# Hybrid encoder block on one core: t stores issued seven half products behind, accumulators copied at the end of their own product, a fifth hi buffer, and a PSUM copy of the rounded part for every weight operand

## The chip, the cores and the metric

The kernel runs on one core of one Trainium2 chip, as one program. The time is device microseconds of that core. The kernel before was run three times: the median is 2214.05 us, the lowest 2213.38 us, the highest 2215.1 us. One more execution was profiled; the engine rows and the trace are of that one.

## What is computed

One layer of a hybrid encoder in float32, for 512 tokens of width 2048: a normalisation and one input projection whose columns feed three head groups (stick-breaking attention, a convolution module, a spatial gating module), a per-head normalisation, an output projection with residual, and then the feed-forward part, in which most of the time lies:

```python
h = rms_norm(x, ffn_norm[l])
gate = causal_depthwise_conv(jnp.einsum('bsd,df->bsf', h, w_gate[l]), ffn_conv_w[l], ffn_conv_b[l])   # 3 taps
up = jnp.einsum('bsd,df->bsf', h, w_up[l])
x = x + jnp.einsum('bsf,fd->bsd', jax.nn.silu(gate) * up, w_down[l])                                   # d_ff = 5632
return rms_norm(x, final_norm)
```

## The kernel before, in words

**Split operands.** TensorE multiplies in a rounded float32 format. Each operand is therefore split in two: `hi` is the rounded value, a cast on ScalarE (ACT), and `lo = src - hi` is the remainder, a subtraction on VectorE (DVE). `mm3` (line 276) adds three matmuls: hi·hi, hi·lo, lo·hi. The weights are split as they come in: `w_split` (line 250) for the input and output projections, `make_split` (line 1022) for gate and up, `dn_split` (line 1180) for down. All three take their hi tile from a ring `whi` of four buffers and their lo tile from a ring `wlo` of four.

**Stages.** Input projection, convolution and attention work run until about 590 us of the span, the output projection until 771 us, gate and up from 771 to 1725 us, down and the last normalisation until the end.

**Gate and up.** There are 44 groups of 256 columns, in turn of w_gate and of w_up (44 = 22 pairs of a gate group and an up group). Each group is one Strassen-like product: seven products over half-size blocks (`SEQ`, line 990), each in two halves over the contraction. Such a half product is called a unit here: 14 units in a group, numbered 0 to 13, 12 matmuls of 256 columns each, on the weight operands L11 (units 0, 1), S1 (2, 3), L12 (4, 5), S3 (6, 7), S2 (8, 9), S4 (10, 11), L22 (12, 13). An L operand is raw weight from a DMA buffer (`b_raw`); an S operand is a sum that GpSimd (POOL) makes (`make_sum`, line 1008) into a ring of three tiles (`b_sum`). The other side of the matmul (`ra`, `rb`, `rc`, `rd`) is the split activation, made once.

The remainder of an S operand, and of L11, is taken from a second copy of the rounded value: ACT casts once to the hi tile in SBUF and once to a PSUM tile `b_hp`, and DVE subtracts the PSUM copy. For L12 and L22 there is only the one cast, and DVE reads both inputs from SBUF:

```python
if (i == 0 and g > 0) or SEQ[i][0] in SUMS:
    hp = zz("b_hp").rearrange("p (k c) -> p k c", k=4)
    act_.copy(hi, src)
    act_.copy(hp.bitcast(F32R), src)
    vec.tensor_tensor(out=lo, in0=src, in1=hp, op=ALU.subtract)
else:
    split(hi, lo, src)
```

**Accumulators.** A group has two PSUM banks (`pt`) of two halves each: X and Y in the first, Z1 and Z2 in the second. The seven products accumulate into X, Z1, Y, Z2, X, Z1, Z2. `product` (line 1078) issues the matmuls and, behind certain products, the copies and additions into two SBUF tiles `ff_g` (c11, c12 in the first, c21, c22 in the second; ring `tmp_g` of eight). Matmuls into one half of a bank wait for reads of either half that were issued before them.

**Outputs.** `gate_out` (line 1046) multiplies a gate tile by a row of norms, runs the three-tap convolution (one ACT operation, two DVE operations that read SBUF twice, `ff_c`) and the SiLU on ACT, and one multiplication on POOL. `up_out` (line 1068) multiplies the up tile by it on POOL (`ff_g<-ff_g,ff_c`), and ACT's queue then issues its store to the DRAM tensor `t`. Both are generators: `run_steps` (line 1118) advances each by one `yield` per unit, which sets how many units behind each step stands.

**Order.** The loop at line 1221 issues, for each unit, the sum of six units ahead, the split of four units ahead, the unit's matmuls and the output steps. A scheduler then orders each engine's instructions by its own estimate of when they are ready; ACT keeps the order of the code. The order that came out is what each engine executes, each engine in its own queue, one behind the other.

Of the kernel before, what the change touches and what calls it, by code (L numbers as in the profile page):

```python
# [9 lines left out]
F32 = mybir.dt.float32  # L10
F32R = mybir.dt.float32r  # L11
# [3 lines left out]
P = 128  # L15
S = 512
# [4 lines left out]
NF = DFF // P  # L21
# [4 lines left out]
TAPS = 31  # L26
# [87 lines left out]
def trunk_kernel(  # L114
# [16 lines left out]
    act_, vec, pool = iss.scalar, iss.vector, iss.gpsimd  # L131

    const = ctx.enter_context(tc.tile_pool(name="const", bufs=1))
    up_stage, gating_stage = ExitStack(), ExitStack()
    wp = ctx.enter_context(tc.tile_pool(name="wp", bufs=3))
# [7 lines left out]
    def s2k(name, dt=F32):  # L143
        return sb.tile([P, S], dt, tag="s2k", bufs=NS2K, name=name)
# [41 lines left out]
    ident = const.tile([P, P], F32, name="ident")  # L186
    make_identity(nc, ident)

    rows_m = const.tile([16, P], F32, name="rows_m")
    nc.scalar.dma_start(out=rows_m, in_=mix_norm[0].rearrange("(k p) -> k p", p=P))  # L190

    def columns(rows, n, name):
# [41 lines left out]
    def w_load(i):  # L234
        if i < len(plan):
            src, k0, nk, c0, ncol = plan[i]
            raws[i] = wp.tile([P, nk, ncol], F32, tag="raw", bufs=3, name="w_raw")
            nc.sync.dma_start(
                out=raws[i],
                in_=src[k0 * P : (k0 + nk) * P, c0 : c0 + ncol].rearrange("(k p) c -> p k c", p=P),  # L240
            )

    def split(hi, lo, src, hi_eng=None, lo_eng=None):
        if hi_eng is None:
            act_.copy(hi, src)
        else:
            hi_eng.tensor_copy(hi, src)
        return (lo_eng or vec).tensor_tensor(out=lo, in0=src, in1=hi.bitcast(F32), op=ALU.subtract)

    def w_split(j):  # L250

        i, s = divmod(j, 2)
        if i >= len(plan):
            return
        nk, ncol = plan[i][2] // 2, plan[i][4]
        hi = wp.tile([P, nk, ncol], F32R, tag="whi", bufs=4, name="w_hi")
        lo = wp.tile([P, nk, ncol], F32R, tag="wlo", bufs=4, name="w_lo")
        iss.now -= 1.5
        split(hi, lo, raws[i][:, s * nk : (s + 1) * nk, :])
        iss.now += 1.5  # L260
        halves[j] = (hi, lo)
        if s == 1:
            del raws[i]
            w_load(i + 3)
# [16 lines left out]
    def proj_t(h, hook=None):  # L281

        banks = [mm("pt") for _ in range(2)]
        for kt in range(KT):
            kk = kt % 2
            if kk == 0:
                hi, lo = w_next()
            for m in range(2):
                cs = slice(m * P, (m + 1) * P)
                mm3(banks[m], hi[:, kk, cs], lo[:, kk, cs], h[kt][0], h[kt][1], kt == 0, kt == KT - 1)  # L290
                if m == 0:
                    iss.tick()
            if kk == 0:
                w_ahead()
            if hook:
                hook(kt)
            iss.tick()
        return banks
# [104 lines left out]
    for b in range(4):  # L403
# [2 lines left out]
            nc.sync.dma_start(out=xblk[b][tt], in_=x[tt * P : (tt + 1) * P, b * S : (b + 1) * S])  # L406
        if b < 3:
            w_load(b)
    rows_a = const.tile([48, P], F32, name="rows_a")
    for i, v in enumerate((merge_norm, ffn_norm)):  # L410
        nc.sync.dma_start(out=rows_a[16 * i : 16 * i + 16, :], in_=v[0].rearrange("(k p) -> k p", p=P))
    for i, v in enumerate((conv_b, conv_ln_g, conv_ln_b, sg_v_norm)):
        nc.sync.dma_start(out=rows_a[32 + 4 * i : 36 + 4 * i, :], in_=v[0].rearrange("(k p) -> k p", p=P))
    rows_c = const.tile([TAPS * 4, P], F32, name="rows_c")
    nc.sync.dma_start(out=rows_c, in_=conv_w[0].rearrange("k (c p) -> (k c) p", p=P))
    rows_f = [const.tile([2 * NF, P], F32, name=f"rows_f{i}") for i in range(2)]
    nc.sync.dma_start(out=rows_f[0], in_=ffn_conv_w[0, 0:2].rearrange("k (c p) -> (k c) p", p=P))
    nc.sync.dma_start(out=rows_f[1][0:NF, :], in_=ffn_conv_w[0, 2].rearrange("(c p) -> c p", p=P))
    nc.sync.dma_start(out=rows_f[1][NF : 2 * NF, :], in_=ffn_conv_b[0].rearrange("(c p) -> c p", p=P))
# [149 lines left out]
    def by_row(banks, name):  # L569
        res = [s2k(name) for _ in banks]  # L570
        for m, t in enumerate(res):
            w = vec.tensor_tensor(out=t, in0=banks[m], in1=row1[0], op=ALU.mult)
        return res, w

    for half in range(2):
# [4 lines left out]
        a_sb, _ = by_row(banks, "cv_a")  # L580
# [261 lines left out]
    for half in range(2):  # L842
        u, _ = by_row(proj_t(hT, first_operands if half else None), "sg_u")
# [35 lines left out]
    def blk_load(g):  # L879
        if g < len(groups):  # L880
            src, c0 = groups[g]
            for h in range(2):
                for q in range(2):
                    t = raw_pool.tile([P, 4, 256], F32, tag="raw", bufs=6, name="b_raw")
                    k0 = (8 * h + 4 * q) * P
                    nc.sync.dma_start(
                        out=t, in_=src[k0 : k0 + 4 * P, c0 : c0 + 256].rearrange("(k p) c -> p k c", p=P)
                    )
                    blk[g, h, q] = t
# [26 lines left out]
    def halves_of(t):  # L916
        return t[:, 0:HT], t[:, HT:S]
# [40 lines left out]
    for nb in range(4):  # L958
# [32 lines left out]
    SEQ = (  # L991
        ("L11", "R11"), ("S1", "T1"), ("L12", "R21"), ("S3", "T3"), ("S2", "T2"), ("S4", "R22"), ("L22", "T4"),
    )
# [6 lines left out]
    def operand(g, name, q):  # L1000
        return raw_block(g, name, q) if name[0] == "L" else sums[g, name, q]

    SUMS = {
        "S1": ("L21", "L22", ALU.add), "S3": ("L11", "L21", ALU.subtract),
        "S2": ("S1", "L11", ALU.subtract), "S4": ("L12", "S2", ALU.subtract),
    }
# [15 lines left out]
    def make_split(n):  # L1022
        g, i, q = UNITS[n]
        if i == 0 and q == 0 and g > 0:
            blk_load(g + 1)
        hi = wp.tile([P, 4, P], F32R, tag="whi", bufs=4, name="b_hi")
        lo = wp.tile([P, 4, P], F32R, tag="wlo", bufs=4, name="b_lo")
        src = operand(g, SEQ[i][0], q)
        if (i == 0 and g > 0) or SEQ[i][0] in SUMS:


            hp = zz("b_hp").rearrange("p (k c) -> p k c", k=4)
# [5 lines that stand above are left out]
        parts[n] = (hi, lo)  # L1038
# [29 lines left out]
    def up_out(f, c):  # L1068
        yield
        pool.tensor_tensor(out=c, in0=c, in1=sil.pop(f), op=ALU.mult)  # L1070
        yield
        yield
        nc.scalar.dma_start(out=t_dram[f // 2][:, f % 2, :], in_=c)

    AHEAD, SUM_AHEAD = 4, 6
# [2 lines left out]
    def product(n):  # L1078
        g, i, q = UNITS[n]
        if g not in banks_of:  # L1080
            b1, b2 = mm("pt"), mm("pt")
            banks_of[g] = (*halves_of(b1), *halves_of(b2))
        X, Y, Z1, Z2 = banks_of[g]
        acc = (X, Z1, Y, Z2, X, Z1, Z2)[i]
        hi, lo = parts.pop(n)
        for kk in range(4):
            rh, rl = R[SEQ[i][1], 4 * q + kk]
            mm3(acc, hi[:, kk, :], lo[:, kk, :], rh, rl, i < 2 and q == 0 and kk == 0, q == 1 and kk == 3)
        if q == 0:
            return  # L1090
        if i < 2:
            return
        if g not in outs_of:
            outs_of[g] = (tmp_g("ff_g0"), tmp_g("ff_g1"))
        (c11, c12), (c21, c22) = (halves_of(c) for c in outs_of[g])
        f0 = 2 * (g // 2)
        out_fn = gate_out if g % 2 == 0 else up_out
        if i == 2:
            act_.copy(c11, X)
            vec.tensor_tensor(out=c11, in0=c11, in1=Y, op=ALU.add)  # L1100
        elif i == 3:
            vec.tensor_copy(c22, Z1)
            vec.tensor_tensor(out=c22, in0=c22, in1=Z2, op=ALU.add)
        elif i == 4:
            u_of[g] = tmp("ff_u")[:, 0:HT]
            act_.copy(u_of[g], X)
            vec.tensor_tensor(out=c22, in0=c22, in1=X, op=ALU.add)
        elif i == 5:
            vec.tensor_tensor(out=c12, in0=u_of[g], in1=Z1, op=ALU.add)
            out_steps.append(out_fn(f0, outs_of[g][0]))  # L1110
        elif i == 6:
            vec.tensor_tensor(out=c21, in0=u_of[g], in1=Z2, op=ALU.add)
            out_steps.append(out_fn(f0 + 1, outs_of[g][1]))
# [66 lines left out]
    def dn_split(j):  # L1180
        i, s = divmod(j, 2)
        if i >= len(dplan):
            return
        if j < n_steps:
            hi = wp.tile([P, S], F32R, tag="whi", bufs=4, name="w_hi")
            lo = wp.tile([P, S], F32R, tag="wlo", bufs=4, name="w_lo")
        else:
            hi, lo = big("w_hi"), big("w_lo")
        split(hi, lo, raw_d[i][:, s, :])
        halves_d[j] = (hi, lo)  # L1190
        if s == 1:
            del raw_d[i]
            dn_load(i + 5)
# [50 lines left out]
    for kg in range(4):  # L1244
        for nb in range(4):
# [4 lines left out]
            for f in range(10 * kg, 10 * kg + 10):  # L1250
# [8 lines left out]
                hi, lo = halves_d.pop(j)  # L1259
# [12 lines left out]
    rstd3, add3, _ = token_stats("o", lambda: dp.tile([P, S], F32, tag="junk", bufs=2, name="junk"))  # L1272
    ms3 = const.tile([P, NT, 4], F32, name="ms3")
    for tt in range(NT):
        ts_ = slice(tt * P, (tt + 1) * P)
        for nb in range(4):
            bank = mm("pl") if tt % 2 == 0 else zz("pl")
            for f in range(4):
# [3 lines left out]
                hi, lo = halves_d[n_steps + 4 * nb + f]  # L1282
# [49 lines left out]
```

## Time and profile before

| | |
|---|---|
| median of three runs | 2214.05 us (2213.38 to 2215.1) |
| the profiled execution, its time | 2215.32 us |
| its span on the core | 2213.6 us |
| gate and up stage within the span | 771 to 1725 us |
| granted TensorE clock, mean | 0.997 |

The span is the time from the first to the last instruction on the core, 1.7 us less than the time of that execution. A busy share is the time in which an engine had an instruction in work, over a stretch. Matmuls overlap each other by their pipeline, so a TensorE that is "busy" all the time is not one that works without gaps: the distance between the starts of neighbouring matmuls tells more. A wait is put down to the instruction that ended last before the waiting one began. PEld is TensorE's weight load, which overlaps its matmuls.

### The profile page before, as it was taken

The numbers are of one execution on the slowest core, as the hardware profiler recorded it, in microseconds if no ns is written. First come the engines' busy times: TensorE is split into PE (matmuls) and PEld (weight loads), VectorE is DVE, ScalarE is ACT, GpSimd is POOL, SyncE is SP. The second block draws the span as 40 slices with busy tenths as digits, with TensorE's granted clock in tenths as the row PEclk, the third lists the DMA queues.
The fourth block names the chain that finished last, engine by engine and source line by source line (L and its number), as shares of the span: only waits on it lengthen the run. The fifth ranks groups of instructions, "written<-read, shape, count | busy, mean of one in ns | idle before, by whom it ended". The sixth has DMA issues, their size and how long they took to land.

```text
span 2213.6 us, 36107 instructions
## 1 busy us (share of the span) xinstructions
PE 2141.4 (97%) x13529; PEld 1930.4 (87%) x13529; DVE 1512.9 (68%) x2264; ACT 1244.8 (56%) x2346; POOL 794.8 (36%) x691
## 2 busy tenths in 40 slices
PE   8999999999999989999999999999999999999998
PEld 6888888898788889999999999999999888888886
DVE  4789897986744687877787887788778534343335
ACT  5335567777633477767676676767667423232223
POOL 2011232322200266576666657766666000000002
PEclk9999999999999999999999999999999999999999
DMA  5322222222264323333324333332433834332232
GB/s 179 95 87 85 62 72 68 67 62 68 77 209 137 119 88 98 113 109 111 125 87 134 100 112 117 104 125 92 128 108 109 307 116 138 108 134 95 95 114 77
DMA packets 190720, 245.27 MB, mean 111 GB/s; under 512 B 8549, under 2 KB 140497, under 8 KB 190545
## 3 DMA queue, kind: packets, MB, share of 16 engines
q1 hardware_dynamic: 183649, 231.16, 32.6%
q10 hardware_dynamic: 6896, 11.81, 1.4%
q8 instruction: 106, 1.74, 0.3%
q14 instruction: 69, 0.57, 0.1%
HBM read 223.01 MB, written 19.92 MB: 110 GB/s over the span
## 4 chain that ended last, share of the span: by engine, by line
PE 77%; DVE 11%; ACT 4%; issue 4%; DMA 1%; POOL 1%; SPq 0%; DVEq 0%; ACTq 0%; POOLq 0%
PE pt L172 43%; PE pd L172 19%; PE po L172 7%; DVE b_lo L105 4%; PE pn L172 3%; PE pl L172 2%; DVE cv_acc L105 1%; DVE w_lo L105 1%; ACT b_hp L105 1%; DVE ff_g L105 1%; ACT e L105 1%; PE av L172 1%; PE z_C L172 1%; PE z_A L172 1%; PE z_B L172 0%
## 5 line engine op out<-in xcount | busy, mean ns | idle before, releaser
L105 DVE TENSOR_TENSOR w_lo<-w_raw,w_hi 128x512 fp32r<-128x512 f32 x400 | 285.8, 720 | 349.2 <-ACT w_hi L105 344.1
L105 ACT CAST w_hi<-w_raw 128x512 fp32r<-128x512 f32 x400 | 245.3, 620 | 465.2 <-PE pd L172 303.5
L105 DVE TENSOR_TENSOR b_lo<-b_sum,b_hp 128x512 fp32r<-128x512 f32 x352 | 237.2, 684 | 167.0 <-ACT b_hp L105 151.3
L105 POOL TENSOR_TENSOR b_sum<-b_raw 128x512 f32<-128x512 f32 x176 | 234.7, 1362 | 245.4 <-DVE w_lo L105 140.0
L105 ACT CAST b_hi<-b_sum 128x512 fp32r<-128x512 f32 x352 | 217.1, 617 | 161.6 <-PE pt L172 110.3
L105 DVE TENSOR_TENSOR b_lo<-b_raw,b_hi 128x512 fp32r<-128x512 f32 x178 | 252.1, 1434 | 26.7 <-ACT b_hi L105 26.6
L172 PE MATMUL pd<-w_lo,t_hi 128*128 128x512 f32 x640 | 249.1, 389 | 0.2 <-DVE w_lo L105 0.2
L172 PE MATMUL pd<-w_hi,t_hi 128*128 128x512 f32 x640 | 249.0, 389 | 0.0
L172 PE MATMUL pd<-w_hi,t_lo 128*128 128x512 f32 x640 | 249.0, 389 | 0.0
L172 PE MATMUL pt<-ra_hi,b_lo 128*128 128x256 f32 x704 | 205.9, 292 | 32.2 <-DVE b_lo L105 32.2
L105 ACT CAST b_hi<-b_raw 128x512 fp32r<-128x512 f32 x264 | 163.2, 619 | 120.4 <-PE pt L172 55.4
L105 ACT CAST b_hp<-b_sum 128x512 fp32r<-128x512 f32 x352 | 205.3, 583 | 0.7 <-DVE x L105 0.7
L172 PE MATMUL pt<-rc_hi,b_hi 128*128 128x256 f32 x704 | 201.4, 286 | 2.5 <-DVE ff_g L105 1.0
L105 POOL TENSOR_TENSOR b_sum<-b_raw,b_sum 128x512 f32<-128x512 f32 x88 | 148.1, 1702 | 151.6 <-DVE b_lo L105 151.6
L172 PE MATMUL pt<-rc_hi,b_lo 128*128 128x256 f32 x704 | 201.4, 286 | 0.0
L172 PE MATMUL pt<-rb_hi,b_lo 128*128 128x256 f32 x704 | 199.4, 283 | 0.6 <-DVE b_lo L105 0.6
L172 PE MATMUL pt<-rb_lo,b_hi 128*128 128x256 f32 x704 | 199.2, 283 | 0.0
L172 PE MATMUL pt<-rb_hi,b_hi 128*128 128x256 f32 x704 | 199.2, 283 | 0.0
L172 PE MATMUL pt<-ra_hi,b_hi 128*128 128x256 f32 x704 | 199.2, 283 | 0.0
L172 PE MATMUL pt<-rc_lo,b_hi 128*128 128x256 f32 x704 | 199.0, 283 | 0.0
L172 PE MATMUL pt<-ra_lo,b_hi 128*128 128x256 f32 x704 | 198.9, 283 | 0.0
L172 PE MATMUL pt<-hT_hi,w_hi 128*128 128x512 f32 x448 | 175.5, 392 | 0.2
(260 smaller groups left out, 5796.7 us busy)
## 6 DMA issues: line engine op xcount, KB each, us to landing
b_raw<-in_w_gate_dram SPq DMA_DIRECT2D x88, 512.0 KB
b_raw<-in_w_up_dram SPq DMA_DIRECT2D x88, 512.0 KB
w_raw<-in_w_down_dram SPq DMA_DIRECT2D x88, 512.0 KB
w_raw<-in_w_in_dram SPq DMA_DIRECT2D x80, 512.0 KB
w_raw<-in_w_out_dram SPq DMA_DIRECT2D x32, 512.0 KB
t<-ff_g ACTq DMA_DIRECT2D x44, 256.0 KB
t_raw<-t SPq DMA_DIRECT2D x22, 512.0 KB
x<-in_x_dram SPq DMA_DIRECT2D x32, 256.0 KB
```

The source lines that it names most:

```text
L105: ins = f(*a, **k)
L172: return nc.tensor.matmul(o, lhsT=lhsT, rhs=rhs, start=start, stop=stop, skip_group_check=True)
```

## The change

- **Stores.** In `up_out` the store of a t tile is issued seven `yield`s behind the multiplication on POOL; it was two.
- **Accumulators.** The copy of X (c11, by ACT) is issued behind unit 1 and the copy of Z1 (c22, by DVE) behind unit 3, each at the end of its own product; they stood behind units 5 and 7. The `ff_g` tiles are taken from their ring accordingly earlier.
- **Buffers.** The `whi` ring has five buffers. The room comes from five small tiles of gains (`rows_m`, `rows_a`, `rows_c`, `rows_f` twice), which are now cut out of the `s2k` ring of the first stages.
- **PSUM copies.** From the third group on (g > 1) every operand has the PSUM copy `b_hp`, L12 and L22 too; the first two groups have it for the S operands alone.

```diff
-    rows_m = const.tile([16, P], F32, name="rows_m")
+    rows_m = s2k("rows_m")[0:16, 0:P]
...
-        hi = wp.tile([P, nk, ncol], F32R, tag="whi", bufs=4, name="w_hi")
+        hi = wp.tile([P, nk, ncol], F32R, tag="whi", bufs=5, name="w_hi")
...
-        hi = wp.tile([P, 4, P], F32R, tag="whi", bufs=4, name="b_hi")
+        hi = wp.tile([P, 4, P], F32R, tag="whi", bufs=5, name="b_hi")
         lo = wp.tile([P, 4, P], F32R, tag="wlo", bufs=4, name="b_lo")
         src = operand(g, SEQ[i][0], q)
-        if (i == 0 and g > 0) or SEQ[i][0] in SUMS:
+        if g > 1 or SEQ[i][0] in SUMS:
...
     def up_out(f, c):
         yield
         pool.tensor_tensor(out=c, in0=c, in1=sil.pop(f), op=ALU.mult)
-        yield
-        yield
+        for _ in range(7):
+            yield
         nc.scalar.dma_start(out=t_dram[f // 2][:, f % 2, :], in_=c)
...
         if q == 0:
             return
-        if i < 2:
-            return
         if g not in outs_of:
             outs_of[g] = (tmp_g("ff_g0"), tmp_g("ff_g1"))
...
-        if i == 2:
+        if i == 0:
             act_.copy(c11, X)
+        elif i == 1:
+            vec.tensor_copy(c22, Z1)
+        elif i == 2:
             vec.tensor_tensor(out=c11, in0=c11, in1=Y, op=ALU.add)
         elif i == 3:
-            vec.tensor_copy(c22, Z1)
             vec.tensor_tensor(out=c22, in0=c22, in1=Z2, op=ALU.add)
```

The change moves instructions on the engines in three places that the prediction speaks of.

ACT's queue where an up group ends and the next gate group begins. `ff_u` is the copy of X behind unit 9 of the ending group; the casts under it are of the next group's L11 and S1; the DMA is the store of the first t tile of the ending group. Before:

```order
L105 COPY ff_u_13515<-pt_13322 128x256
L105 CAST b_hi_13528<-b_raw_13229 128x512
L105 CAST b_hp_13530<-b_raw_13229 128x512
L105 CAST b_hi_13547<-b_raw_13231 128x512
L105 CAST b_hp_13549<-b_raw_13231 128x512
L1073 DMA t_9_7714<-ff_g0_13438 128x512
L105 CAST b_hi_13566<-b_sum_13518 128x512
```

In the changed kernel:

```order
L105 COPY ff_u_13655<-pt_13456 128x256
L105 CAST b_hi_13668<-b_raw_13361 128x512
L105 CAST b_hp_13670<-b_raw_13361 128x512
L105 CAST b_hi_13687<-b_raw_13363 128x512
L105 CAST b_hp_13689<-b_raw_13363 128x512
L105 CAST b_hi_13706<-b_sum_13658 128x512
L105 CAST b_hp_13708<-b_sum_13658 128x512
L105 CAST b_hi_13725<-b_sum_13658 128x512
L105 CAST b_hp_13727<-b_sum_13658 128x512
L1073 DMA t_9_7714<-ff_g0_13490 128x512
L105 CAST b_hi_13746<-b_raw_13365 128x512
L105 CAST b_hp_13748<-b_raw_13365 128x512
```

The store now stands behind the casts of both S1 halves, and L12 (the last two rows) has a second cast.

TensorE's queue at such a border. `rb` is unit 11 of the ending group, `rd` its unit 12, and the `ra` rows between them are matmuls of the next group's unit 0, which the scheduler puts ahead. Before:

```order
L172 MATMUL pt_13611<-rb_hi_7907,b_lo_13745 128x256
L172 MATMUL pt_13894<-ra_hi_6720,b_hi_13809 128x256
L172 MATMUL pt_13894<-ra_lo_6721,b_hi_13809 128x256
L172 MATMUL pt_13894<-ra_hi_6720,b_lo_13810 128x256
L172 MATMUL pt_13894<-ra_hi_6786,b_hi_13809 128x256
L172 MATMUL pt_13894<-ra_lo_6787,b_hi_13809 128x256
L172 MATMUL pt_13894<-ra_hi_6786,b_lo_13810 128x256
L172 MATMUL pt_13611<-rd_7484,b_hi_13764 128x256 x2
```

In the changed kernel:

```order
L172 MATMUL pt_13457<-rb_hi_7907,b_lo_13600 128x256
L172 MATMUL pt_13752<-ra_hi_6720,b_hi_13668 128x256
L172 MATMUL pt_13752<-ra_lo_6721,b_hi_13668 128x256
L172 MATMUL pt_13752<-ra_hi_6720,b_lo_13669 128x256
L172 MATMUL pt_13752<-ra_hi_6786,b_hi_13668 128x256
L172 MATMUL pt_13752<-ra_lo_6787,b_hi_13668 128x256
L172 MATMUL pt_13752<-ra_hi_6786,b_lo_13669 128x256
L172 MATMUL pt_13752<-ra_hi_6850,b_hi_13668 128x256
L172 MATMUL pt_13752<-ra_lo_6851,b_hi_13668 128x256
L172 MATMUL pt_13752<-ra_hi_6850,b_lo_13669 128x256
L172 MATMUL pt_13752<-ra_lo_6925,b_hi_13668 128x256
L172 MATMUL pt_13457<-rd_7484,b_hi_13619 128x256 x2
```

Eleven matmuls of the next group stand ahead of unit 12 where six did. The twelfth of that unit follows behind unit 13.

DVE's queue in the first half of an up group, while the convolution of the gate group ahead of it runs. `SCALAR_TENSOR_TENSOR` is a tap of that convolution, `b_lo` a remainder, `ff_g<-ff_g,pt` the addition of Y to c11 behind unit 5. Before:

```order
L105 TENSOR_TENSOR b_lo_13930<-b_sum_13888,b_hp_13931 128x512
L105 SCALAR_TENSOR_TENSOR ff_c_13887<-ff_g1_13723,cols_f0_539,ff_c_13887 128x511
L105 SCALAR_TENSOR_TENSOR ff_c_13887<-ff_g1_13723,cols_f0_539,ff_c_13887 128x510
L105 TENSOR_TENSOR b_lo_13951<-b_sum_13888,b_hp_13952 128x512
L105 TENSOR_TENSOR b_lo_13972<-b_sum_13927,b_hp_13973 128x512
L105 TENSOR_TENSOR b_lo_13993<-b_sum_13927,b_hp_13994 128x512
L105 TENSOR_TENSOR ff_g0_14010<-ff_g0_14010,pt_13894 128x256
```

In the changed kernel:

```order
L105 TENSOR_TENSOR b_lo_14085<-b_sum_14036,b_hp_14086 128x512
L105 SCALAR_TENSOR_TENSOR ff_c_13996<-ff_g0_13786,cols_f0_539,ff_c_13996 128x510
L105 TENSOR_TENSOR b_lo_14106<-b_sum_14036,b_hp_14107 128x512
L105 COPY ff_g1_14079<-pt_14045 128x256
L105 SCALAR_TENSOR_TENSOR ff_c_14035<-ff_g1_13787,cols_f0_539,ff_c_14035 128x511
L105 TENSOR_TENSOR b_lo_14128<-b_sum_14082,b_hp_14129 128x512
L105 SCALAR_TENSOR_TENSOR ff_c_14035<-ff_g1_13787,cols_f0_539,ff_c_14035 128x510
L105 TENSOR_TENSOR b_lo_14149<-b_sum_14082,b_hp_14150 128x512
L105 TENSOR_TENSOR ff_g0_14078<-ff_g0_14078,pt_14044 128x256
```

The last two taps stood ahead of the remainder of S3's second half (`b_lo_13951`); they now stand behind it (`b_lo_14106`) and behind the copy of Z1.

## Rows read from the trace of the kernel before

**Rows 1.** The page, part 1: busy time, share of span, instructions per engine

```profile
PE 2141.4 (97%) x13529; PEld 1930.4 (87%) x13529; DVE 1512.9 (68%) x2264; ACT 1244.8 (56%) x2346; POOL 794.8 (36%) x691
```

**Rows 2.** Windows: us; busy per engine (instructions); granted clock, DMA share, GB/s

```profile
771.00:1725.00 954.00, 916.76 (x7419) 897.31 (x7419) 750.75 (x1040) 669.59 (x1259) 624.09 (x453) 1.00 0.36 112
1800.00:2000.00 200.00, 200.00 (x884) 165.60 (x883) 81.22 (x126) 55.90 (x93) 0.00 (x0) 1.00 0.36 120
```

**Rows 3.** Waits of the whole trace: who for whom, us in total, times, longest

```profile
ACT b_hi L105 <- PE pt L172: 165.7, 157, 4.1
...
PE pt L172 <- DVE b_lo L105: 32.8, 66, 2.1
...
PE av L172 <- DVE wt_lo L105: 6.7, 10, 1.5
```

**Rows 4.** Timeline of PE over one period: start, us, operation, [idle before]

```profile
1163.61 0.39 PE L172 MATMUL pt<-ra_hi,b_lo 128*128 128x256 f32 x1 [0.55 <-DVE b_lo L105]
...
1169.94 0.38 PE L172 MATMUL pt<-ra_hi,b_lo 128*128 128x256 f32 x1 [0.32 <-DVE b_lo L105]
...
1185.22 0.38 PE L172 MATMUL pt<-ra_hi,b_lo 128*128 128x256 f32 x1 [0.63 <-DVE b_lo L105]
...
1202.76 0.28 PE L172 MATMUL pt<-rb_hi,b_hi 128*128 128x256 f32 x1
...
1205.76 0.28 PE L172 MATMUL pt<-ra_lo,b_hi 128*128 128x256 f32 x1
1206.58 0.38 PE L172 MATMUL pt<-ra_hi,b_lo 128*128 128x256 f32 x1 [0.55 <-DVE b_lo L105]
```

**Rows 5.** Lines: the remainder from SBUF, and the cast to PSUM

```profile
L105 DVE TENSOR_TENSOR b_lo<-b_raw,b_hi 128x512 fp32r<-128x512 f32 x178 | 252.1, 1434 | 26.7 <-ACT b_hi L105 26.6
...
L105 ACT CAST b_hp<-b_raw 128x512 fp32r<-128x512 f32 x86 | 50.3, 585 | 0.0
```

**Rows 6.** Timeline of DVE and ACT at the border at 1206 us

```profile
1202.11 3.49 DVE L105 TENSOR_TENSOR b_lo<-b_raw,b_hi 128x512 fp32r<-128x512 f32 x2 [0.40 <-ACT b_hi L105]
1205.86 0.68 DVE L105 TENSOR_TENSOR b_lo<-b_raw,b_hp 128x512 fp32r<-128x512 f32 x1
...
1204.32 0.62 ACT L105 CAST b_hi<-b_raw 128x512 fp32r<-128x512 f32 x1 [0.54 <-ACT ff_u L105]
1204.85 0.59 ACT L105 CAST b_hp<-b_raw 128x512 fp32r<-128x512 f32 x1
```

**Rows 7.** Timeline of POOL, ACT's queue and ACT, same border

```profile
1209.19 1.29 POOL L105 TENSOR_TENSOR ff_g<-ff_g,ff_c 128x512 f32<-128x512 f32 x1
...
1210.52 0.33 ACTq L1073 DMA_DIRECT2D t<-ff_g  x1
1210.94 0.62 ACT L105 CAST b_hi<-b_sum 128x512 fp32r<-128x512 f32 x1 [4.07 <-PE pt L172]
```

**Rows 8.** Timeline of DVE, POOL and PEld in the next up group's half

```profile
1191.41 1.78 DVE L105 SCALAR_TENSOR_TENSOR ff_c<-ff_g,cols_f,ff_c 128x511 f32<-128x511 f32 x1
1193.12 1.78 DVE L105 TENSOR_TENSOR b_lo<-b_raw,b_hi 128x512 fp32r<-128x512 f32 x1
1194.82 0.74 DVE L105 SCALAR_TENSOR_TENSOR ff_c<-ff_g,cols_f,ff_c 128x510 f32<-128x510 f32 x1
1196.08 1.53 DVE L105 SCALAR_TENSOR_TENSOR ff_c<-ff_g,cols_f,ff_c 128x511 f32<-128x511 f32 x2
1197.52 1.88 DVE L105 TENSOR_TENSOR b_lo<-b_sum,b_hp 128x512 fp32r<-128x512 f32 x3
1199.32 0.42 DVE L105 TENSOR_TENSOR ff_g<-ff_g,pt 128x256 f32<-128x256 f32 x1
...
1191.04 3.31 POOL L105 TENSOR_TENSOR b_sum<-b_raw,b_sum 128x512 f32<-128x512 f32 x2 [7.35 <-DVE b_lo L105]
1198.28 2.55 POOL L105 TENSOR_TENSOR b_sum<-b_raw 128x512 f32<-128x512 f32 x2 [3.93 <-DVE b_lo L105]
...
1199.79 0.19 PEld L172 LDWEIGHTS pt<-rc_hi,b_hi 128*128 128x128 f32 x1 [0.29 <-DVE ff_g L105]
```

More of the change, by code (lines that the diff above doesn't have):

```diff
@@ L408, in trunk_kernel @@
             w_load(b)
-    rows_a = const.tile([48, P], F32, name="rows_a")
+    rows_a = s2k("rows_a")[0:48, 0:P]
     for i, v in enumerate((merge_norm, ffn_norm)):
@@ L413, in trunk_kernel @@
         nc.sync.dma_start(out=rows_a[32 + 4 * i : 36 + 4 * i, :], in_=v[0].rearrange("(k p) -> k p", p=P))
-    rows_c = const.tile([TAPS * 4, P], F32, name="rows_c")
+    rows_c = s2k("rows_c")[0 : TAPS * 4, 0:P]
     nc.sync.dma_start(out=rows_c, in_=conv_w[0].rearrange("k (c p) -> (k c) p", p=P))
-    rows_f = [const.tile([2 * NF, P], F32, name=f"rows_f{i}") for i in range(2)]
+    rows_f = [s2k(f"rows_f{i}")[0 : 2 * NF, 0:P] for i in range(2)]
     nc.sync.dma_start(out=rows_f[0], in_=ffn_conv_w[0, 0:2].rearrange("k (c p) -> (k c) p", p=P))
@@ L1184, in dn_split @@
         if j < n_steps:
-            hi = wp.tile([P, S], F32R, tag="whi", bufs=4, name="w_hi")
+            hi = wp.tile([P, S], F32R, tag="whi", bufs=5, name="w_hi")
             lo = wp.tile([P, S], F32R, tag="wlo", bufs=4, name="w_lo")
```

## The prediction

> **What bounds the kernel now.** I read the busy shares first: TensorE is busy for 97% of the span, no other engine for more than 68% [rows 1]. Its clock is full in both long stages, and the DMA share is 0.36 [rows 2], so neither throttle nor memory sets the pace. In the down stage TensorE is busy for 200 us of 200 [rows 2]: the fifth buffer that its split gets as well has nothing to win there. What can be won lies in gate and up.
>
> There the timeline repeats. The same event, the last early matmul of a next up-to-gate border, comes at 1163.61 and 1206.58 [rows 4]: one gate group and one up group take 42.97 us. Without waits, 25 matmuls from 1202.76 to 1205.76 take 3.00 us [rows 4], 0.120 each; the 2 x 14 x 12 = 336 matmuls of a period need 40.32. So **2.65 us of a period are lost**, in 21 periods (44 groups without the first two) 56 us.
>
> The places, in order of time [rows 4]: the border up to gate (0.55 idle), 6.3 us behind it (0.32), the border gate to up (0.63), then the next border. These marks understate: from the matmul at 1205.76 to the one at 1206.58 are 0.82, less a pitch 0.70. A fourth is unit 8 of the up group, where a weight load waits for DVE's addition of Y to c11, 0.29 [rows 8]. In the list of waits TensorE's for b_lo are 32.8 us in 66 cases, three per period [rows 3].
>
> Why b_lo is late at a border: DVE is in two remainders read from SBUF, those of L22, for 3.49 us until 1205.60, and takes the next group's L11 only at 1205.86, though ACT's cast of it to PSUM was done at 1205.44 [rows 6]. Why it is late 6.3 us behind: ACT's queue holds the store of t, which waits for POOL's multiplication until 1210.48; ACT idles 4.07 us and casts S1 only at 1210.94 [rows 7].
>
> **The change part by part.**
>
> *PSUM copies.* By the orders of the instructions 166 of 178 SBUF remainders become PSUM ones. One costs 1.434 us on average [rows 5], and 1.78 while POOL works [rows 8]; from PSUM it is 0.68, or 0.60 from start to start [rows 6, 8]. DVE is relieved of 166 x 0.75 = 125 us. ACT gets 166 casts of 0.585 [rows 5], 97 us: its busy time in the stage goes from 670 to 767 of 954 us [rows 2]. Two L22 remainders take 1.2 instead of 3.5, so the L11 remainder can come some 2 us earlier, given its cast. The cast waits for a hi buffer, and the fifth is the one that comes free a unit earlier, 1.44 us (12 x 0.120). Both border stalls are covered by that. What covers them is that DVE has room; if it has none, they return.
>
> *Stores.* Five units later, 7.2 us, POOL's multiplication, done by 1210.48 [rows 7], is long past, and the store stands behind the casts of S1. ACT's 4.07 idle goes and with it the stall behind the border. What stands behind the store now, L12's casts, has four units of lead.
>
> *Accumulators copied earlier.* No more instructions; ACT's and DVE's copies fall where their results are ready. The eleven early matmuls at a border (six before) need no more than the earlier remainder. Unit 12, now behind them, waits for nothing new by my replay.
>
> *The addition of Y at unit 8 of the up group.* It grows, and is the new wait. TensorE's unit 8 writes X, in the bank that the addition reads. On DVE the last two taps now stand behind the remainder of S3's second half. That remainder frees a tile of the b_sum ring, which lets POOL start S1's two sums of the next group (2.55 for two [rows 8]): so both taps meet POOL. What that does can be seen once before the change: POOL's two sums, begun at 1191.04, take 3.31 instead of 2.55, and the tap begun at 1191.41 takes 1.78 instead of 0.74. They took turns: sum, tap, sum, remainder [rows 8].
>
> I replayed this half by hand with an unstalled TensorE, time zero at unit 10 of the gate group, so that unit 12 follows the eleven early matmuls at 4.20 and unit 8 of the up group is due at 17.28. With 0.60 for a remainder, 0.72 for a tap, 1.27 for a sum and 0.42 for an addition [rows 8]: the remainder of S3's second half ends at 13.7, the copy of Z1 at 14.15, the first sum at 15.0, the tap at 15.7, the second sum at 17.0, a remainder between them at 16.3, the last tap at 17.7, one more remainder at 18.3, the addition at 18.7. TensorE then waits about **1.45 us** per period. With 1.78 for both taps regardless of POOL's turns it would be 1.9. Without any meeting the addition ends at 17.15, no wait. I take 1.45, because the trace shows the turns [rows 8]; 0 and 1.9 stay as ends.
>
> The Trainium skill ("SBUF — State Buffer", section "Who interferes with whom") has the shared port pair as an exclusive lock between GpSimd and a VectorE instruction that reads SBUF twice, and none for one that reads SBUF once. By that rule turns are complete, 1.45, and the trace agrees as far as it goes (1.78 against 0.74, and 0.68 for a remainder from PSUM); by the flat row it would be 1.9.
>
> *Small ones.* At the start, gain rows come out of a ring, so SP issues one weight load earlier; it could cost or give up to 1.6 us by its place ahead of x. I take 0, since later weight loads gate the projection. In attention the wait of 6.7 us in total for DVE's wt_lo [rows 3] could lose or gain with the shifted schedule; 0 taken. The first two groups keep their form; their longest wait, 2.1 us [rows 3], may go or double.
>
> **Sum.** Of 2.65 us, 1.45 stay: 1.20 x 21 = 25 us. The profiled execution took 2215.3, so 2190; the median is 1.3 below that, so **2189 us**. With the wait at 1.9 it is 0.75 x 21 = 16, 2198; with +-8 for the small ones and for stalls that shorten but don't go, 2176 to 2198 is the forecast's own range.
>
> **Rivals.**
>
> *All stalls go.* If the scheduler's order gives the taps a gap, for instance because TensorE's slower start shifts POOL, all 2.65 x 21 = 56 us come back: 2158. For it: POOL needs only 624 of 954 us [rows 2], and one sum starting 1.3 us later removes a meeting. Against it: what starts POOL is the very remainder ahead of the taps.
>
> *Unit 8 eats most.* If a third DVE instruction meets POOL there (another turn of 1.27 less slack), the wait is 2.2 or more, and 0.45 x 21 = 9 us or less stay: 2200 to 2209.
>
> *The stall moves, no change.* The borders are relieved but ACT's casts come as late as DVE's remainders did: each lost 0.7 comes back, 2210 to 2218.
>
> *ACT becomes the bound, slower.* Per period ACT is busy 670/22.2 = 30.2 us now and 8 casts more make 34.8 of 42.97, the rest being 8.2. It waits for TensorE in 157 cases for 165.7 us [rows 3], 7.5 per period, since hi buffers come free only as TensorE reads. These fit into 8.2 barely; from there on ACT decides. With a fifth buffer the waits should shrink. Should they grow by a quarter to 9.4, the period is 34.8 + 9.4 = 44.2, 1.25 x 21 = 26 us slower: 2240. Against it: a wait for a free buffer is slack, not work; an ACT that is late waits less.
>
> *The change does not do what it says.* The orders exclude it: 12 SBUF remainders are left, and store, copies and casts stand where the text has them.
>
> **How the numbers follow.** Forecast 0.50 (2176 to 2198); all stalls go 0.20 (2158, or lower by the 6.7 of attention); unit 8 eats most 0.15, which counts as faster down to 2209; no change 0.07; slower 0.08. The range from 2153 to 2207 takes the first two whole and most of the third. Faster by over 0.2% (4.4 us, about what a measurement of this kernel tells from none): 0.50 + 0.20 + 0.15 = 0.85; same 0.07; slower 0.08.
>
> **What would show it.** Right: TensorE's idle marks before the early matmuls at both borders are gone; SBUF remainders are 12; ACT's 4.07 before the S1 cast is gone; the weight load at unit 8 of the up group waits for ff_g by 1.4 us a period; two taps a period take 1.7 or so; a period is 41.8. Wrong: TensorE waits for b_lo again with ACT busy just before (ACT bound), a period of 40.4 (all go), or a longer wait at unit 12.

## The result, and the profile after

The changed kernel takes 2192.7 us, the median of four runs (2188.19 to 2194.81), against 2214.57 us before (four runs): a ratio of 0.9897, with a 95% interval from 0.9878 to 0.9916. It is 21.9 us faster. The profiled execution took 2191.24 us, with a span of 2189.5; the spans differ by 24.1.

Busy time per engine after (page, part 1), to be held against [rows 1]:

```profile
PE 2128.5 (97%) x13529; PEld 1930.4 (88%) x13529; DVE 1422.2 (65%) x2264; ACT 1329.0 (61%) x2512; POOL 755.3 (34%) x691
```

The windows of [rows 2] after the change:

```profile
771.00:1725.00 954.00, 925.87 (x7526) 913.60 (x7525) 664.79 (x1060) 767.35 (x1445) 588.96 (x454) 1.00 0.37 121
```

ACT has 98 us more in the stage, DVE 86 less, the clock is the same. The list of waits answers to [rows 3]:

```profile
ACT b_hi L105 <- PE pt L172: 72.9, 198, 2.1
...
PE pt L172 <- DVE ff_g L105: 21.3, 23, 1.7
...
PE pt L172 <- DVE b_lo L105: 4.3, 5, 1.4
```

TensorE's waits for b_lo fell from 32.8 us in 66 cases to 4.3 in 5. In their place it waits for `ff_g`, once per period. PE's timeline over a period, with every row that begins with an idle mark (unit 8 of the up group, the same event twice):

```profile
1108.66 0.36 PE L172 MATMUL pt<-rc_hi,b_hi 128*128 128x256 f32 x1 [0.87 <-DVE ff_g L105]
...
1149.14 0.28 PE L172 MATMUL pt<-rc_hi,b_lo 128*128 128x256 f32 x1
1150.30 0.35 PE L172 MATMUL pt<-rc_hi,b_hi 128*128 128x256 f32 x1 [0.88 <-DVE ff_g L105]
```

A period is 41.64 us, 1.33 less than the 42.97 of [rows 4]. From 1149.14 to 1150.30 are 1.16, less a pitch of 0.12 is 1.04; with 0.08 in the next step, 1.12 are lost there. Two steps of 0.10, at unit 12 of either group, make it 1.32, and 40.32 + 1.32 = 41.64.

How the wait comes about: DVE and POOL ahead of unit 8.

```profile
1103.29 0.67 DVE L105 TENSOR_TENSOR b_lo<-b_sum,b_hp 128x512 fp32r<-128x512 f32 x1
1103.89 0.41 DVE L105 COPY ff_g<-pt 128x256 f32<-128x256 f32 x1
1104.22 1.67 DVE L105 SCALAR_TENSOR_TENSOR ff_c<-ff_g,cols_f,ff_c 128x511 f32<-128x511 f32 x1
1105.81 0.68 DVE L105 TENSOR_TENSOR b_lo<-b_sum,b_hp 128x512 fp32r<-128x512 f32 x1
1106.40 1.18 DVE L105 SCALAR_TENSOR_TENSOR ff_c<-ff_g,cols_f,ff_c 128x510 f32<-128x510 f32 x1
1107.51 0.68 DVE L105 TENSOR_TENSOR b_lo<-b_sum,b_hp 128x512 fp32r<-128x512 f32 x1
1108.11 0.41 DVE L105 TENSOR_TENSOR ff_g<-ff_g,pt 128x256 f32<-128x256 f32 x1
...
1104.04 3.00 POOL L105 TENSOR_TENSOR b_sum<-b_raw 128x512 f32<-128x512 f32 x2 [2.48 <-DVE b_lo L105]
```

S3's remainder ends at 1103.96 and frees the ring; POOL starts its two sums at 1104.04. DVE is then in the copy of Z1 and takes its first tap at 1104.22, 0.18 behind POOL: the tap waits for the first sum (1.67 instead of 0.74), the second tap for the second sum (1.18), and the addition ends at 1108.52.

### The profile page after: what moved, and what is told of

It is laid out like the page before. It is cut to its first block, busy times and chain, and to the rows that moved or that the text cites. A ratio compares the mean times of both kernels' runs of the same rounds, so it can differ in the third digit from the quotient of the medians.

```text
span 2189.5 us, 36332 instructions
## 1 busy us (share of the span) xinstructions
PE 2128.5 (97%) x13529; PEld 1930.4 (88%) x13529; DVE 1422.2 (65%) x2264; ACT 1329.0 (61%) x2512; POOL 755.3 (34%) x691
## 3 DMA queue, kind: packets, MB, share of 16 engines
q8 instruction: 106, 1.74, 0.3%
## 4 chain that ended last, share of the span: by engine, by line
PE 87%; DVE 5%; ACT 4%; issue 2%; POOL 1%; DMA 0%; SPq 0%; ACTq 0%; POOLq 0%; DVEq 0%
PE pt L172 50%; PE pd L172 20%; PE po L172 8%; PE pn L172 4%; PE pl L172 2%; DVE w_lo L105 1%; ACT e L105 1%; DVE cv_acc L105 1%; PE av L172 1%; PE ps_tr L176 1%; PE z_C L172 1%; PE z_A L172 1%; DVE wt_lo L105 0%; PE z_B L172 0%; ACT b_hi L105 0%
## 5 line engine op out<-in xcount | busy, mean ns | idle before, releaser
L105 DVE TENSOR_TENSOR b_lo<-b_raw,b_hp 128x512 fp32r<-128x512 f32 x252 | 170.9, 685 | 87.8 <-PE pt L172 70.4
L172 PE MATMUL pt<-ra_hi,b_lo 128*128 128x256 f32 x704 | 199.7, 284 | 3.0 <-DVE b_lo L105 3.0
L105 POOL TENSOR_TENSOR b_sum<-b_raw,b_sum 128x512 f32<-128x512 f32 x88 | 123.5, 1415 | 212.1 <-DVE b_lo L105 212.1
```

Source lines behind the costliest of these rows:

```text
L105: ins = f(*a, **k)
L172: return nc.tensor.matmul(o, lhsT=lhsT, rhs=rhs, start=start, stop=stop, skip_group_check=True)
```

## The experiments

The theory to begin with was the prediction's: PSUM copies cure the borders, late stores the stall behind them, both taps meeting POOL make the wait at unit 8. The rival: the fifth buffer cures the borders. Four runs undo one part each; eight more put the parts together otherwise. Each was timed beside the kernel before, whose medians there are 2214.8 to 2215.83.

**e1, the SBUF remainders back.**

```diff
-        if g > 1 or SEQ[i][0] in SUMS:
+        if (i == 0 and g > 0) or SEQ[i][0] in SUMS:
```

> The changed kernel with the SBUF remainders of L12 and L22 back (before's condition); stores, early accumulator copies and fifth buffer stay. Theory (DVE's SBUF remainders make the border stalls): both border stalls of 0.89 and 0.90 us per period return, and unit 8 still waits; 1.8 x 21 = 38 us over the changed kernel's 2192.7, about 2230, TensorE waits for b_lo twice per period. Rival (the fifth buffer cured the borders, the copies do little): under 0.4 us per period, 2193 to 2201, b_lo waits stay away.

Measured 2193.89 us, ratio 0.9901 (0.9888 to 0.9915): 1.2 us from the changed kernel. No wait for b_lo at a border. Within the change as it stands, the theory fell and the rival held.

**e2, the stores at two half products.**

```diff
-        for _ in range(7):
-            yield
+        yield
+        yield
         nc.scalar.dma_start(out=t_dram[f // 2][:, f % 2, :], in_=c)
```

> The changed kernel with the store of t two half products behind again. Theory (the store blocks ACT's casts of S1): the stall 6.3 us behind the border returns with 0.58 us per period, 0.58 x 21 = 12 us, 2205, and ACT idles about 4 us before a cast of S1. Rival (with five hi buffers the casts stand ahead far enough): 2193 and no b_lo wait there.

Measured 2193.18 us, 0.99 (0.9887 to 0.9914): no difference, no stall. ACT's timeline of this run shows why:

```profile
1114.43 0.62 ACT L105 CAST b_hi<-b_sum 128x512 fp32r<-128x512 f32 x1 [0.33 <-PE pt L172]
1114.96 0.58 ACT L105 CAST b_hp<-b_sum 128x512 fp32r<-128x512 f32 x1
1115.59 0.33 ACTq L1073 DMA_DIRECT2D t<-ff_g  x1
```

The store stands behind S1's casts with two half products as it does with seven. The order is the scheduler's, not the code's, for ACT's stores too (the description of the kernel ahead says that ACT keeps the order of the code; that is wrong).

**e3, four hi buffers.** The edit is `bufs=4` in the three `whi` lines.

> The changed kernel with four hi buffers. Theory (the copies cure most of the border, the buffer the rest): L11's cast waits for the end of unit 10, two casts and a remainder take 1.7 to 1.9 us against the 1.44 of unit 11, so 0.4 per border comes back, 0.8 x 21 = 17 us, less what unit 8 gains because the order has the taps earlier (up to 1.1 x 21 = 23): 2186 to 2210. Rival (the buffer alone cures the borders): both stalls of 0.9 return, 38 us, less the same: 2207 to 2231.

Measured 2212.74 us, 0.9989 (0.998 to 0.9997): 20 us of the gain of 21.9 are gone; a period takes 42.61 us. Not by both 0.9 stalls. The borders keep 0.43 each, as the theory had it; 0.38, from start to start less the pitch, are lost behind the border up to gate; and a new wait, 0.92 and 0.11 in the next step, stands at unit 4, whose product Y shares its bank with X. PE's timeline at that border, behind it and at unit 4, and ACT's queue and ACT there:

```profile
1122.16 0.39 PE L172 MATMUL pt<-ra_hi,b_lo 128*128 128x256 f32 x1 [0.17 <-DVE b_lo L105]
...
1128.29 0.39 PE L172 MATMUL pt<-ra_hi,b_lo 128*128 128x256 f32 x1
...
1131.93 0.38 PE L172 MATMUL pt<-rb_hi,b_hi 128*128 128x256 f32 x1 [0.76 <-ACT ff_g L105]
...
1125.92 0.33 ACTq L1073 DMA_DIRECT2D t<-ff_g  x1
1126.35 0.62 ACT L105 CAST b_hi<-b_sum 128x512 fp32r<-128x512 f32 x1 [3.52 <-POOL ff_g L105]
...
1131.52 0.36 ACT L105 COPY ff_g<-pt 128x256 f32<-128x256 f32 x1
```

With four buffers the store again stands ahead of S1's casts, ACT is late, and its early copy of X holds up unit 4. So the total lies 2.7 us above the theory's range and in the rival's, but the new wait was in neither.

**e4, the accumulator copies late again.**

```diff
+        if i < 2:
+            return
...
-        if i == 0:
+        if i == 2:
             act_.copy(c11, X)
-        elif i == 1:
-            vec.tensor_copy(c22, Z1)
-        elif i == 2:
...
+            vec.tensor_copy(c22, Z1)
```

> The changed kernel with the copies of X and Z1 behind units 5 and 7 again. Theory (they are no part of the gain; the copy of Z1 now stands ahead of the taps and delays the addition at unit 8): that wait shrinks by 0.4 per period, 8 us faster, about 2184, or no change. Rival (early copies are needed to free the banks): waits at units 4 to 8 grow, by 0.5 or more per period, over 2203.

Measured 2166.13 us, 0.9774 (0.976 to 0.9787): 26.6 us faster than the changed kernel, three times the 8 expected. No wait is left in a period of 40.53 us. DVE and POOL at the same place:

```profile
1137.16 0.67 DVE L105 TENSOR_TENSOR b_lo<-b_sum,b_hp 128x512 fp32r<-128x512 f32 x1
1137.76 0.74 DVE L105 SCALAR_TENSOR_TENSOR ff_c<-ff_g,cols_f,ff_c 128x511 f32<-128x511 f32 x1
1138.42 0.67 DVE L105 TENSOR_TENSOR b_lo<-b_sum,b_hp 128x512 fp32r<-128x512 f32 x1
1139.02 1.19 DVE L105 SCALAR_TENSOR_TENSOR ff_c<-ff_g,cols_f,ff_c 128x510 f32<-128x510 f32 x1
...
1140.73 0.41 DVE L105 TENSOR_TENSOR ff_g<-ff_g,pt 128x256 f32<-128x256 f32 x1
...
1137.91 1.74 POOL L105 TENSOR_TENSOR b_sum<-b_raw 128x512 f32<-128x512 f32 x1 [2.48 <-DVE b_lo L105]
```

Without the copy between them the tap begins at 1137.76, 0.15 ahead of POOL's sum, and takes 0.74; this time POOL waits (1.74 instead of 1.3). From the start of the remainder to the end of the addition are 3.98 us, against 5.23 in the changed kernel: 0.33 of copy and 0.93 of a lost turn. The expectation had only the 0.4. The period is 1.11 us shorter; 21 of them make the 23.3 us by which the spans of the two profiled executions differ (2189.5 and 2166.2). The medians differ by 3.3 more, which is within the spread of the single times.

**e5, the copy of Z1 alone late.** X's copy stays behind unit 1.

```diff
-        elif i == 1:
-            vec.tensor_copy(c22, Z1)
...
         elif i == 3:
+            vec.tensor_copy(c22, Z1)
             vec.tensor_tensor(out=c22, in0=c22, in1=Z2, op=ALU.add)
```

> The changed kernel with the copy of Z1 alone behind unit 7 again; the copy of X stays early. Theory (the early copy of Z1 stands on DVE between the remainder of S3 and the taps, 0.33 us, and so POOL's sum gets its turn ahead of both taps): the wait at unit 8 goes, 2166, a period of 40.5 us. Rival (ACT's early copy of X is what delays the addition): 2193, wait unchanged.

Measured 2166.99 us, 0.9782 (0.9768 to 0.9797). The period is again 40.53 us. It is Z1's copy on DVE; X's on ACT costs nothing here.

**e6, the second gate tile's taps three half products later**, with both copies early.

```diff
+        for _ in range(3 * (f % 2) if f > 1 else 0):
+            yield
         for k in (1, 0):
```

> The changed kernel with the two taps of the second gate tile three half products later (from the third group on), so that DVE's addition of Y stands ahead of the last tap; everything else as changed. Theory (the taps that meet POOL delay the addition): one turn instead of two, the addition ends some 1.2 us earlier, wait at unit 8 gone, 2166 to 2172. Rival (the addition waits for something else, such as ACT's copy of X or the unit before it): 2193.

Measured 2170.2 us, 0.9799 (0.9784 to 0.9813). The addition now precedes the last tap, and from the third group on TensorE has no wait for it:

```profile
1135.14 0.68 DVE L105 TENSOR_TENSOR b_lo<-b_sum,b_hp 128x512 fp32r<-128x512 f32 x1
...
1136.67 1.08 DVE L105 SCALAR_TENSOR_TENSOR ff_c<-ff_g,cols_f,ff_c 128x511 f32<-128x511 f32 x1
1137.66 0.41 DVE L105 TENSOR_TENSOR ff_g<-ff_g,pt 128x256 f32<-128x256 f32 x1
```

From the start of the remainder to the end of the addition are 2.93 us, against 5.23. The taps that meet POOL were the delay.

**e7, the kernel before with the fifth buffer alone** (all three `whi` lines to `bufs=5`, the gain rows cut out of the `s2k` ring as in the change).

> The kernel before with the fifth hi buffer (and the gain rows cut out of the ring, which makes its room) and nothing else. Theory now (the buffer cures all three b_lo stalls by itself, PSUM copies and stores do nothing beside it): the gain of the run without early copies, 2166, up to 2175 if SBUF remainders of L12 meet POOL ahead of unit 8. Rival (buffer and copies are both needed, DVE's 3.49 us at the border stays): 0.9 us at one or both borders, 2185 to 2204.

Measured 2187.68 us, 0.9879 (0.9864 to 0.9893): 27 us faster, all three b_lo stalls gone (0.1 at most at a border), yet 22 us short of e4. The border gate to up, in the kernel before (ACT, DVE) and in this run (ACT, DVE):

```profile
1181.44 0.62 ACT L105 CAST b_hi<-b_raw 128x512 fp32r<-128x512 f32 x1 [0.82 <-PE pt L172]
...
1180.66 3.58 DVE L105 TENSOR_TENSOR b_lo<-b_raw,b_hi 128x512 fp32r<-128x512 f32 x2 [0.17 <-ACT b_hi L105]
...
1184.49 0.67 DVE L105 TENSOR_TENSOR b_lo<-b_raw,b_hp 128x512 fp32r<-128x512 f32 x1
```

```profile
1086.52 0.62 ACT L105 CAST b_hi<-b_raw 128x512 fp32r<-128x512 f32 x1 [0.82 <-PE pt L172]
...
1086.65 3.28 DVE L105 TENSOR_TENSOR b_lo<-b_raw,b_hi 128x512 fp32r<-128x512 f32 x2
...
1090.19 1.46 DVE L105 TENSOR_TENSOR b_lo<-b_raw,b_hp 128x512 fp32r<-128x512 f32 x2
```

TensorE wants L11's remainder at 1090.94 (before: at 1184.43, the mark's 1185.22 less the loss of 0.79). L22's two still take 3.28 us, but their casts have a free buffer a unit earlier: the second one starts 4.42 us ahead of that moment, before 2.99. So L11's remainder starts 0.75 ahead of it and not 0.06 behind, and its first half is done in time. The move of the gain rows has no visible part in it: with four buffers a border loses 0.43 with the rows moved (e3) and without (e8).

What is left is unit 8. L12's SBUF remainder (1.76) and the row multiplication (1.77) each wait for POOL, a tap further on for POOL's next sum (1.42), DVE is late with all that follows, and unit 8 waits again. DVE, then PE:

```profile
1096.62 1.76 DVE L105 TENSOR_TENSOR b_lo<-b_raw,b_hi 128x512 fp32r<-128x512 f32 x1
1098.30 1.77 DVE L105 TENSOR_TENSOR ff_g<-ff_g,row_x 128x512 f32<-128x512 f32 x1
...
1103.72 1.42 DVE L105 SCALAR_TENSOR_TENSOR ff_c<-ff_g,cols_f,ff_c 128x510 f32<-128x510 f32 x1
...
1105.09 0.28 PE L172 MATMUL pt<-rc_hi,b_lo 128*128 128x256 f32 x1
1106.11 0.39 PE L172 MATMUL pt<-rc_hi,b_hi 128*128 128x256 f32 x1 [0.74 <-DVE ff_g L105]
```

So the buffer cures the borders alone; the copies are needed for what shows behind that. Each side of the expectation had half.

**e8, copies and stores without the fifth buffer**, accumulators late.

> The kernel before with the PSUM copies and the late stores, with four hi buffers and the old accumulator copies. First theory (copies and stores alone cure most): 0.4 us left per border and 0.35 behind it, 1.3 of 2.65 us gained per period, 28 us, 2187. Rival (the hi buffer is the limit whatever DVE does): within 10 us of the kernel before, 2205 to 2215.

Measured 2185.84 us, 0.987 (0.9854 to 0.9886). As the first theory had it, 0.43 stay at each border; the 0.35 behind it, which the theory also kept, did not show.

**e9, the stores alone**, on the kernel before.

> The kernel before with the stores seven half products behind and nothing else (four hi buffers, SBUF remainders). First theory (the store holds ACT's casts of S1 and makes the stall 6.3 us behind the border): 0.58 us per period goes, 12 us, 2203. Rival (the casts of S1 are late there anyway): 2210 to 2215.

Measured 2215.05 us, 0.9998 (0.9989 to 1.0007). Nothing. ACT's timeline shows the store where it was in [rows 7], with the same idle time:

```profile
1211.19 0.33 ACTq L1073 DMA_DIRECT2D t<-ff_g  x1
1211.62 0.62 ACT L105 CAST b_hi<-b_sum 128x512 fp32r<-128x512 f32 x1 [4.07 <-PE pt L172]
```

This says that the edit does not move the store, not that the store costs nothing.

**e10, the copies alone**, on the kernel before.

> The kernel before with the PSUM copies and nothing else: four hi buffers, stores two half products behind. If the copies alone made the gain of copies and stores together: 2186, borders 0.43 each, nothing behind them. If the stores are needed for the third stall: 0.58 x 21 = 12 us more, 2198, with ACT idle about 4 us in the store's wait.

Measured 2188.53 us, 0.9875 (0.986 to 0.989): the gain of e8 to within 2.7 us, less than the spread of this run's own times (2186.04 to 2190.01). The store is still ahead of S1's casts, but the stall behind the border is down to 0.07. POOL before, up to the multiplication of [rows 7], then POOL and ACT in this run:

```profile
1202.04 3.01 POOL L105 TENSOR_TENSOR b_sum<-b_raw 128x512 f32<-128x512 f32 x2
1205.02 1.72 POOL L105 TENSOR_TENSOR ff_c<-ff_c,row_x 128x512 f32<-128x512 f32 x1
```

```profile
1109.99 2.55 POOL L105 TENSOR_TENSOR b_sum<-b_raw 128x512 f32<-128x512 f32 x2
1112.50 1.31 POOL L105 TENSOR_TENSOR ff_c<-ff_c,row_x 128x512 f32<-128x512 f32 x1
1113.77 2.54 POOL L105 TENSOR_TENSOR b_sum<-b_sum,b_raw 128x512 f32<-128x512 f32 x2
1116.25 1.31 POOL L105 TENSOR_TENSOR ff_g<-ff_g,ff_c 128x512 f32<-128x512 f32 x1
...
1117.59 0.33 ACTq L1073 DMA_DIRECT2D t<-ff_g  x1
1118.01 0.62 ACT L105 CAST b_hi<-b_sum 128x512 fp32r<-128x512 f32 x1 [3.19 <-PE pt L172]
```

The multiplication that the store waits for starts 2.55 us behind the last matmul ahead of the border's wait (1113.70); before it was 3.43 (1205.76 to 1209.19). With no SBUF remainders on DVE, POOL is less held up (2.55 and 1.31 for what took 3.01 and 1.72), and the store lets go 0.9 earlier: ACT idles 3.19 instead of 4.07.

**e11, fifth buffer and copies**, stores at two half products, accumulators late.

> The kernel before with fifth buffer and PSUM copies; stores two half products behind and accumulator copies late. If stores play no part once there are five buffers: 2166, a period of 40.5 us without waits. If they do (the run with early accumulator copies hid it in the wait at unit 8): the third stall returns with 0.3 to 0.6 us per period, 2172 to 2179.

Measured 2164.93 us, 0.9773 (0.9759 to 0.9786), without a wait in the period. With five buffers the stores play no part.

**e12, the best version:** late accumulator copies, PSUM copies from the second group on (`g > 0`), the rest as changed.

> The changed kernel with the accumulator copies late and the PSUM copies from the second group on (g > 0) instead of from the third. Theory (the periods have no wait left, only the first two groups do): the waits at 820 to 822 us, 0.8 and 1.0, shorten; 2163 to 2166. Rival (ACT is the engine that is late there): up to 3 us more, 2169.

Measured 2162.7 us, 0.9762 (0.9748 to 0.9775), the fastest of all: 30 us below the changed kernel. Of the 4.4 us of span to e11, about 2.4 come from the first two groups, where TensorE's wait at the border at about 820 us is 0.19 instead of 0.84 and one of 0.95 behind it is gone; 2.0 us had been gained before the stage starts (769.6 against 771.6), which no run here explains.

Together, medians in us. A period, from unit 12 to the same unit a pair of groups later, takes 42.97 us before, 41.5 with either the fifth buffer or the PSUM copies (e7, e8, e10), 40.53 with both and Z1's copy late (e4, e5, e11, e12), 41.64 in the changed kernel and 42.61 in e3.

| hi buffers | remainders | copies of X, Z1 | stores | us |
|---|---|---|---|---|
| 4 | SBUF | late | 2 | 2214.57 (before) |
| 4 | SBUF | late | 7 | 2215.05 |
| 4 | PSUM | late | 2 / 7 | 2188.53 / 2185.84 |
| 5 | SBUF | late | 2 | 2187.68 |
| 5 | PSUM | late | 2 / 7 | 2164.93 / 2166.13 |
| 4 | PSUM | early | 7 | 2212.74 |
| 5 | SBUF | early | 7 | 2193.89 |
| 5 | PSUM | early | 2 / 7 | 2193.18 / 2192.7 (the change) |

## Why the prediction was right, and where it was wrong

The total came out as the likeliest case had it: 2189 predicted, 2192.7 measured. The places of the loss in the period were the right ones, both borders and the stall behind vanished, and the new wait came at unit 8 of the up group, by the addition behind two taps that meet POOL's sums. The wait was predicted at 1.45 and is 1.12; with the two steps of 0.10 it is 1.32 that stay, so a period gave 1.33 instead of 1.20. The replay had 5.0 us from the end of S3's remainder to the end of the addition; the trace has 4.56.

The first two groups, taken at no change, gave some back: by unit 8 of the second up group the changed kernel is 1.9 us late, 0.6 of it from the start of the stage (771.6 against 771.0). PE at unit 8 of the second and of the last up group, before and after:

```profile
856.98 0.38 PE L172 MATMUL pt<-rc_hi,b_hi 128*128 128x256 f32 x1
...
1714.83 0.39 PE L172 MATMUL pt<-rc_hi,b_hi 128*128 128x256 f32 x1
```

```profile
858.87 0.35 PE L172 MATMUL pt<-rc_hi,b_hi 128*128 128x256 f32 x1 [0.88 <-DVE ff_g L105]
...
1691.22 0.35 PE L172 MATMUL pt<-rc_hi,b_hi 128*128 128x256 f32 x1 [0.57 <-DVE ff_g L105]
```

Between the two the change gains 25.5 us, which leaves 23.6 of the 24.1 by which the spans differ. The shorter wait and the loss at the start go opposite ways; that the sum came out so close is in part luck. Nor do the first two groups quite "keep their form": the old condition gave L11 of the second group a PSUM copy, the new one doesn't. In e1, which has the old condition, the stretch from the start of the stage to unit 8 of the second up group takes 86.90 us (771.30 to 858.20) instead of 87.23; no run takes that copy back alone.

So the path and the wait that stays were right for the change as a whole. Three steps put the gain on the wrong parts.

*"PSUM copies ... Both border stalls are covered by that."* Within the change they are worth 1.2 us (e1). The fifth buffer, which the prediction had as a helper for the cast, cures all three stalls alone (e7), and the copies alone nearly do (e8, e10): two remedies for one stall. Either alone gives 27 us (e7, e10, each against its own runs of before), both 50.6 (e11), because the second then removes what stands next, the wait at unit 8 or the last 0.43 of each border.

*"Stores. ... ACT's 4.07 idle goes and with it the stall."* The idle went, but not by this edit: seven half products instead of two leave the store where it was (e2, e9), and the fifth buffer moves S1's casts ahead of it (e7 has no stall there). The prediction compared the orders of the whole change, and gave what it saw to the edit that seemed to aim at it.

*"Accumulators copied earlier. No more instructions"*, costed at nothing. This edit costs 27 us, more than the change gains: 2166.13 without it, 2192.7 with it. The hand replay had the copy of Z1 in it and so had the wait, but the wait was put down to the taps' new place. A second replay, without the copy, would have asked which of DVE and POOL goes first when 0.33 us are taken out; the prediction made only the one of the whole change. With four buffers the edit costs as much by another way (2185.84 against 2212.74): by the traces of e8 and e3, 1.03 more per period at unit 4 for X's copy on ACT and 0.38 behind the border, less some 0.3 that e8 loses elsewhere; the period goes from 41.49 to 42.61.

The relief of DVE was forecast at 125 us. The remainders from raw weights went from 310.5 to 181.2 us, 129 less; but taps and row multiplications, which now meet POOL, took 26 more (119.1 to 145.5), and all of DVE 91 less. ACT's 97 came as 98, and it did not become the bound: it waits for TensorE 72.9 us where it waited 165.7 [rows 3].

The Trainium skill ("SBUF — State Buffer", section "Who interferes with whom") adds to its lock that the order of issue decides who blocks, not the shape of the operation. The traces agree: a tap 0.18 us behind POOL's sum takes 1.67, one 0.15 ahead of it takes 0.74 and the sum 1.74. The flat price of 1.78 for both taps, the other end in the prediction, did not show: they took 1.67 and 1.18.

## What to carry to other kernels

When a change has several edits, replay the timeline with each left out, not only the sum of all: two edits that cure the same stall hide each other, and one that is "only moved" can cost all that the rest brings. Where operations of two engines take turns, as DVE's taps and POOL's sums do here, ask of every one that moves which of the two is now first, and by how many hundredths. And see in the orders of each edit alone whether it moves the instruction at all; a distance written in the code is only a wish where a scheduler sets the order.

## What the runs showed that was not expected

How much a lead of 0.2 us decides: 0.33 us of a copy on DVE turned into 1.25 us of delay in every period (5.23 against 3.98 from S3's remainder to the addition) and a period longer by 1.11, 23 us in 21 periods. And that SBUF remainders on DVE slow POOL so far that a store in ACT's queue lets go 0.9 us later, though neither engine is near its limit (DVE 750.75, POOL 624.09 of 954 us [rows 2]).
